# Two layers of a streaming encoder on one core: the adaLN sums, their buffers and the residual affine are placed anew

## The chip, the cores and the metric

The kernel runs on one core of one Trainium2 chip. The metric is the device time of one execution in microseconds. The engines are TensorE (PE in the profile; its weight loads are PEld), VectorE (DVE), ScalarE (ACT), GpSimd (POOL) and SyncE (SP), each with a queue of its own that it works through in order. DMAs are issued from such a queue too: a DMA whose buffer isn't free yet holds everything behind it on that queue.

## The reference

Two layers over 512 tokens of width 1024, all in float32. In each layer three sublayers follow one another, and each is modulated by a vector `c`:

```python
mod = (c_act @ ada_w[l] + ada_b[l]).reshape(b, N_SUB, 3, 1, D_MODEL)
h = modulate(x, mod[:, 0, 0], mod[:, 0, 1])              # x * (1 + scale) + shift
y = swiglu_ffn(h, ffn1_w_in[l], ffn1_w_out[l])
x = layer_norm(ALPHA * x + 0.5 * mod[:, 0, 2] * y, ln_g[l, 0], ln_b[l, 0])
...
x = layer_norm(ALPHA * x + mod[:, 1, 2] * y, ln_g[l, 1], ln_b[l, 1])
...
x = layer_norm(ALPHA * x + 0.5 * mod[:, 2, 2] * y, ln_g[l, 2], ln_b[l, 2])
```

The first and the third sublayer are SwiGLU networks with an inner width of 2816, the "half-steps". The second is a mixer of three head groups: a Mamba-2 scan, an attention with forgetting, and a gated short convolution. What `mod` gives each sublayer, shift, scale and gate, comes from a product of `silu(c)` with `ada_w`, 1024 by 9216 in each layer.

## The kernel before

**Sections.** The six sublayers are the sections 0 to 5; 0, 2, 3 and 5 are FFNs (`ffn`), 1 and 4 mixers (`mixer`). The residual stream `xt` stays in SBUF as four tiles of 128 tokens; its modulated and transposed form `hT` is the operand of the projections.

**Products in three passes.** Every float32 product is made of three float32r matmuls (`mm3`): each operand is split into a high part (ACT copies it: `hi`, `hh`, `ah`, `gh`) and a low part (VectorE subtracts: `li`, `hl`, `al`, `gl`). Weights are loaded as raw tiles (`ri`, `ro`, SyncE's queue, two buffers) and split into six high and six low tiles.

**An FFN** runs over 11 pairs of 256 inner columns, in a group of six and one of five. In a pair `cols_unit` loads and splits the weights of gate and of up, then four banks of 24 matmuls each follow (`order`), then `sg` (SiLU, ACT), `af` (product, VectorE), and `ah`, `al`, which stay in the pool `lp` (28 slots, tag "s") until the output projection. After each group `out_proj` multiplies them with the output weights in two halves `h`, and `fold` adds the gated result to `xt`. In the last group the layer norm follows tile by tile, and the next section's `hT` is made by transposes.

**The residual affine.** The norm leaves `xt` without its gain and bias, which the modulation has folded into `modA` and `modB`. For the residual, `x_affine` (line 632) multiplies all four tiles by `lng` and adds `lnb`, 16 instructions of 128x512 on POOL. It runs after pair 1 of an FFN, and in the mixer after `feat(C_C)`. `ln_vectors` (line 364) loads the four vectors, spread over the partitions, from ACT's queue. In section 0 the small parameter rows (`rows_v`, `rows_ln`) follow on the same queue; `columns` transposes them after pair 3 into `vT` and `lnT`.

**adaLN beside the FFN.** The product with `ada_w` is not done on TensorE but on VectorE, beside the FFN. `ada_acc` (line 228) loads eight blocks of 128x1024 (`ra`, pool `adap`, two buffers) and accumulates them in `acc`, weighted by `cT`. `acc_split` (line 246) splits the sum; the high halves `gh` lie in the temporaries `tp` (nine), the low ones `gl` in an `ra` buffer. `acc_sum` (line 257) then sums over the partitions by two matmuls with a matrix of ones, into a bank of the pool `psb` (four banks): `pm` for shift and scale, `pg` for the gate. `ada_ss(s)` makes the scale of section `s` (called `ss<s>.1` below) and its shift (`ss<s>.0`), `ada_gate(s)` its gate (`g<s>`).

These are generators. `begin` puts them in a list: in sections 0 and 3 the gate of the section, then `ss` and gate of the next one, then `ss` of the one after; in sections 2 and 5 the gate and, in 2, `ss` of section 3. `tick` is called twice in each pair, once after the weights of gate and once after those of up, both before the pair's matmuls, and once for each weight unit in `out_proj`. Each tick adds 2.7 credits (sections 0 and 3) or 1.3, and each block takes one. A generator that yields `TICK` ends the tick at once; so split and sum come at different ticks. `drain` runs what is left at a section's end.

**What sets the order.** The program only gives priorities: the framework's scheduler puts the instructions of each engine in an order by its own estimate of when they are ready. `issue_after` (used by `after`) adds a rule of order between two instructions of one engine. `mm_last` is the last instruction of the newest `mm3`.

**The mixer** uses the temporaries for its short-lived tiles: `am` (made on POOL, line 948), `cbm`, `m`, `xw`, `yo`, `prob`, `qa`, the high and low halves `pth` and `ptl`. Its projections (`feat`, 48 matmuls) are put between the steps of the scan and of the attention. It also takes two `ra` buffers for `xdt`.

Of the kernel before, what the change touches and what calls it, by code (L numbers as in the profile page):

```python
# [9 lines left out]
F32R = mybir.dt.float32r  # L10
# [5 lines left out]
P = 128  # L16
# [9 lines left out]
RMS_EPS = 1e-5  # L26
NEG = -1.0e30
NLONG = 28
NTMP = 9
NW = 6  # L30
PAD_W = 16
POS = 1
BPOS = 2
TICK = object()
CR = (2.7, 1.3)
WSZ = 1024

# [32 lines left out]
def trunk(ctx, tc, x, c, ln_in_g, ln_in_b, ada_w, ada_b, ffn1_w_in, ffn1_w_out,  # L70
# [11 lines left out]

    shift("pad0", PAD_W)
    rawp = ctx.enter_context(tc.tile_pool(name="rawp", bufs=2))
    adap = ctx.enter_context(tc.tile_pool(name="adap", bufs=2))
    whp = ctx.enter_context(tc.tile_pool(name="whp", bufs=NW))
    wlp = ctx.enter_context(tc.tile_pool(name="wlp", bufs=NW))
    lp = ctx.enter_context(tc.tile_pool(name="lp", bufs=NLONG))
# [15 lines left out]
    def tmp(shape, name, dt=F32):  # L104
        return tp.tile(shape, dt, tag="t", name=name)
# [30 lines left out]

    def rows_v(l):
        rows = slot([NROW, P], F32, f"rows{l}")
        act.dma_start(rows[0:72, :], ada_b[l].rearrange("(r p) -> r p", p=P))
        act.dma_start(rows[R_CW:R_CB, :], ssd_conv_w[l].rearrange("k (c p) -> (k c) p", p=P))  # L140
        act.dma_start(rows[R_CB:R_SW, :], ssd_conv_b[l].rearrange("(c p) -> c p", p=P))
        act.dma_start(rows[R_SW:R_NG, :], sconv_w[l].rearrange("k (c p) -> (k c) p", p=P))
        act.dma_start(rows[R_NG:NROW, :], ssd_norm_g[l].rearrange("(c p) -> c p", p=P))
        return rows

    def rows_ln():
        rows = slot([96, P], F32, "rowsl")
        act.dma_start(rows[0:48, :], ln_g.rearrange("l j (r p) -> (l j r) p", p=P))
        act.dma_start(rows[48:96, :], ln_b.rearrange("l j (r p) -> (l j r) p", p=P))
        return rows  # L150

    def rows_first():
# [93 lines left out]
    def acc_split(acc):  # L246

        parts = []
        los = adap.tile([P, 2, 512], F32R, tag="ra", name="gl")
        for h in range(2):  # L250
            hi, lo = tmp([P, 512], "gh", F32R), los[:, h]
            act.activation(hi, acc[h], AF.Copy)
            dve.tensor_tensor(lo, acc[h], hi.bitcast(F32), ALU.subtract)
            parts.append((hi, lo))
        return parts

    def acc_sum(ps, hi, lo):

        pe.matmul(ps, onesr, hi, start=True, stop=False)
        pe.matmul(ps, onesr, lo, start=False, stop=True)  # L260

    def new_mod(s):
# [21 lines left out]
    def ada_ss(s):  # L284
        l, j = divmod(s, 3)
        new_mod(s)
        pres = []
        for which in (1, 0):
            acc = None
            for a in ada_acc(l, (j * 3 + which) * D):  # L290
                acc = acc if a is TICK else a
                yield a
            sums = sm.tile([P, KD], F32, tag=f"sums{which}", name=f"sums{which}", bufs=1)
            parts = acc_split(acc)
            yield TICK
            for h in range(2):
                ps = pb([P, 4, P], f"pm{s}_{which}_{h}")
                acc_sum(ps, *parts[h])
                dg = tmp([P, 4, P], "dg")
                dve.tensor_tensor(dg, ps, ident[:, None, :].to_broadcast([P, 4, P]), ALU.mult)  # L300
                dve.tensor_reduce(sums[:, h * 4:h * 4 + 4], dg, axis=AX.X, op=ALU.add)
            pres.append(sums)
        mod_finish(s, 0, KD, *pres)

    FIRST = ((0, 4), (4, 3), (7, 1))
# [40 lines left out]
    def ada_gate(s):  # L346
        l, j = divmod(s, 3)
        col = (j * 3 + 2) * D
        gate = [slot([P, 512], F32, f"gate{s}_{h}") for h in range(2)]
        for h in range(2):  # L350
            sp.dma_start(gate[h], ada_b[l, col + h * 512:col + h * 512 + 512].partition_broadcast(P))
        acc = None
        for a in ada_acc(l, col):
            acc = acc if a is TICK else a
            yield a
        parts = acc_split(acc)
        yield TICK
        for h in range(2):
            ps = pb([P, 512], f"pg{s}_{h}")
            acc_sum(ps, *parts[h])  # L360
            dve.tensor_tensor(gate[h], ps, gate[h], ALU.add)
        gates[s] = gate

    def ln_vectors(s):
        g, b = (ln_in_g, ln_in_b) if s == 0 else (ln_g[(s - 1) // 3, (s - 1) % 3], ln_b[(s - 1) // 3, (s - 1) % 3])
        for n, v in (("g", g), ("b", b)):
            for h in range(2):
                a = slot([P, 512], F32, f"ln{n}{s}_{h}")
                act.dma_start(a, v[h * 512:(h + 1) * 512].partition_broadcast(P))
                aff[s, n, h] = a  # L370

    pending = []
# [3 lines left out]
    def begin(*gens):  # L376
# [2 lines left out]
        credit[0] = 0.0  # L379
        credit[1] = len(pending) and CR[0] if len(gens) > 2 else CR[1]  # L380

    def tick():
        credit[0] += credit[1]
        while pending and credit[0] >= 1:
            try:
                if next(pending[0]) is TICK:
                    break
                credit[0] -= 1
            except StopIteration:
                pending.pop(0)  # L390

# [237 lines left out]
        last[0] = act_last[0]  # L629
        return banks, units[2]  # L630

    def x_affine(s, eng):

        ln_vectors(s)
        for t in range(NT):
            for h in range(2):
                xh = xt[t][:, h * 512:(h + 1) * 512]
                eng.tensor_tensor(xh, xh, aff[s, "g", h], ALU.mult)  # L638
                eng.tensor_tensor(xh, xh, aff[s, "b", h], ALU.add)
# [17 lines left out]
    def by_token(ah, al):  # L657
        return lambda t: (ah[:, t * P:(t + 1) * P], al[:, t * P:(t + 1) * P])

    def ffn(s, w_in, w_out):  # L660
        for gi, grp in enumerate((range(0, 6), range(6, NPAIR))):
            acts = []
            for jp in grp:
                units, banks = [], []
                for which in range(2):
                    if s > 0 or jp > 0:
                        units.append(next_unit if (s, jp, which) == (0, 1, 0) else cols_unit(w_in, which * DFF + jp * 256, f"i{s}_{jp}_{which}", ln_done[0] if s > 0 and jp == 1 else None))
                        banks.append([pa([P, T], f"pf{s}_{jp}_{which}_{j}") for j in range(2)])
                    tick()
                if s == 0 and jp == 0:  # L670
                    banks, order = first_banks, []
                elif jp == 0:
                    order = [(0, KD, a, a + 256, j, which) for a in (0, 256) for which in range(2) for j in range(2)]
                else:
                    order = [(0, KD, 0, T, j, which) for j in range(2) for which in range(2)]
                for i, (ka, kb, a, b, j, which) in enumerate(order):
                    wh, wl = units[which][j]
                    for k in range(ka, kb):
                        mm3(banks[which][j][:, a:b], wh[:, k, :], wl[:, k, :],
                            hT[0][:, k, a:b], hT[1][:, k, a:b], k == 0, k == KD - 1)  # L680
                    if jp == 0 and i == POS:
                        last_tile[0](mm_last[0])
                for j in range(2):
                    sg = tmp([P, T], "sg")
                    act.activation(sg, banks[0][j], AF.Silu)
                    af = tmp([P, T], "af")
                    dve.tensor_tensor(af, sg, banks[1][j], ALU.mult)
                    ah = slot([P, T], F32R, f"ah{s}_{jp}_{j}")
                    al = slot([P, T], F32R, f"al{s}_{jp}_{j}")
                    act_last[0] = act.activation(ah, af, AF.Copy)  # L690
                    dve.tensor_tensor(al, af, ah.bitcast(F32), ALU.subtract)
                    acts.append(by_token(ah, al))
                if jp == 1:
                    x_affine(s, pool)
                    if s == 0:
                        masks()
                        rows = [(vT[0], rows_v(0)), (vT[1], rows_v(1)), (lnT, rows_ln())]
                        small_loads(0)
                        small_loads(1)
                if s == 0 and jp == 3:  # L700
                    for r in rows:
                        columns(*r)
                    neg_a()
            last = gi == 1
            if last:
                if s == 5:
                    ln_vectors(6)
            out_proj(s, w_out, grp[0] * 256, acts, True, not last, last)

    def out_proj(s, w_out, r0, acts, half, first, last):  # L710
# [6 lines left out]
        for h in range(2):  # L717
# [11 lines left out]
            for k in range(nhead):  # L729
                for t in range(NT):  # L730
                    go((k,), banks[t], t)
            for t in range(NT):
                if h == 1 and end == (s, t):
                    for piece in range(2):
# [465 lines left out]
```

## Time and profile before

| what | value |
|---|---|
| median of 3 runs | 2000.05 us (1996.82 to 2003.78) |
| the profiled execution | 2000.76 us, span 1999.0 us |
| granted TensorE clock, mean | 0.995 |
| bytes read from HBM | 260.37 MB |

The span runs from the first to the last instruction of the profiled execution. TensorE's share of busy time is high in every slice, so the views to read are those that show where it stands still: the list of its waits, the timeline at each of them, and windows of a few microseconds, which also give the clock that the throttle granted. One tick of work lasts long enough for a place to be named: in sections 0 and 3 a pair of undisturbed matmuls takes about 22 us. Section 0 reaches to about 418 us, mixer 1 to about 650, section 2 to about 1016, section 3 to about 1397, mixer 4 to about 1628; section 5 is the rest.

### The profile page before, as it was taken

To read this page: it belongs to the slowest core of one execution; us is meant where nothing else is said; L and a number is where in the kernel's file an instruction comes from. 1 tells how busy PE (TensorE), PEld (TensorE's weight loads), DVE (VectorE), ACT (ScalarE), POOL (GpSimd) and SP (SyncE) were. 2 spreads that over 40 slices of the span, in tenths; PEclk is the share of its full clock that TensorE was granted. 3 is DMA by queue.
4 is the path that set the end of the run, shared out by engine and by line. 5 is a ranking of instruction groups with operands and counts; after the bars stand their busy time and mean duration, and the time that the engine had idled before them with its cause. 6 is when DMAs were issued, how large, how long until landed. Compare 5 with 4: busy or idle time off the path is not lost.

```text
span 1999.0 us, 23434 instructions
## 1 busy us (share of the span) xinstructions
PE 1947.5 (97%) x9422; PEld 1627.3 (81%) x9422; DVE 1208.1 (60%) x1770; ACT 690.9 (35%) x1094; POOL 220.6 (11%) x182
## 2 busy tenths in 40 slices
PE   5999999999999999999999999999999999999998
PEld 4777878898878988888898788788978798888887
DVE  8886663477677655543477857435766785433336
ACT  3433223164365432123152322223544553222320
POOL 0230000007100040000005000000260004000000
PEclk9999999999999999999999999999999999999999
DMA  9766542234211544432345746232422144323331
GB/s 327 235 196 225 173 166 82 75 106 127 84 65 53 184 153 163 155 107 93 106 151 188 248 163 229 86 103 57 135 87 83 53 133 142 105 85 106 104 107 43
DMA packets 178605, 263.99 MB, mean 132 GB/s; under 512 B 9676, under 2 KB 124736, under 8 KB 178496
## 3 DMA queue, kind: packets, MB, share of 16 engines
q1 hardware_dynamic: 174000, 254.98, 38.8%
q10 hardware_dynamic: 4496, 7.52, 1.3%
q8 instruction: 74, 1.21, 0.2%
q14 instruction: 35, 0.29, 0.0%
HBM read 260.37 MB, written 2.10 MB: 131 GB/s over the span
## 4 chain that ended last, share of the span: by engine, by line
PE 77%; DVE 11%; DMA 7%; ACT 3%; issue 2%; POOL 0%; POOLq 0%; ACTq 0%; SPq 0%; DVEq 0%
PE pf L53 37%; PE po L53 23%; DMA ra<-in_ada_w_dram 6%; DVE acc L53 4%; PE pz L53 2%; DVE li L53 2%; DVE af L53 1%; PE pjm4x L53 1%; PE pjm1x L53 1%; PE ptr L53 1%; PE pS L53 1%; DMA ri<-in_ffn_w_in_dram 1%; PE py L53 1%; DVE x L53 1%; DVE gy L53 1%
## 5 line engine op out<-in xcount | busy, mean ns | idle before, releaser
L53 PE MATMUL pf<-hh,li 128*128 128x512 f32 (+1 forms) x1504 | 567.8, 378 | 1.4 <-DVE li L53 1.0
L53 PE MATMUL pf<-hl,hi 128*128 128x512 f32 (+1 forms) x1504 | 566.9, 377 | 0.2 <-DVE hl L53 0.2
L53 PE MATMUL pf<-hh,hi 128*128 128x512 f32 (+1 forms) x1504 | 566.9, 377 | 0.0
L53 DVE TENSOR_TENSOR li<-ri,hi 128x1024 fp32r<-128x1024 f32 x176 | 224.7, 1282 | 184.0 <-ACT hi L53 183.8
L53 PEld LDWEIGHTS pf<-hh,li 128*128 128x128 f32 x1504 | 284.4, 189 | 53.4 <-DVE li L53 1.7
L53 PEld LDWEIGHTS pf<-hl,hi 128*128 128x128 f32 x1504 | 284.2, 189 | 52.2 <-DVE hl L53 0.9
L53 PEld LDWEIGHTS pf<-hh,hi 128*128 128x128 f32 x1504 | 284.5, 189 | 51.3
L53 ACT ACTIVATE hi<-ri 128x1024 fp32r<-128x1024 f32 x176 | 185.5, 1060 | 311.1 <-PE pf L53 200.7
L53 PE MATMUL po<-ho,al 128*128 128x512 f32 (+1 forms) x704 | 273.5, 389 | 0.5 <-DVE af L53 0.4
L53 PE MATMUL po<-lo,ah 128*128 128x512 f32 (+1 forms) x704 | 272.9, 388 | 0.0
L53 PE MATMUL po<-ho,ah 128*128 128x512 f32 (+1 forms) x704 | 272.6, 388 | 0.0
L53 DVE TENSOR_TENSOR lo<-ro,ho 128x1024 fp32r<-128x1024 f32 x104 | 127.2, 1223 | 204.5 <-ACT ho L53 204.4
L53 DVE SCALAR_TENSOR_TENSOR acc<-ra,cT,acc 128x512 f32<-128x512 f32 x224 | 172.9, 815 | 67.1 <-DMA ra<-in_ada_w_dram 66.7
L53 ACT ACTIVATE ho<-ro 128x1024 fp32r<-128x1024 f32 x104 | 110.1, 1059 | 286.7 <-PE po L53 160.1
L451 POOL TENSOR_TENSOR rs<-ve,mhalf 128x1 f32<-128x1 f32 x28 | 17.3, 620 | 1277.5 <-DVE ve L53 1276.2
L53 PEld LDWEIGHTS po<-ho,al 128*128 128x128 f32 x704 | 132.2, 188 | 28.2 <-DVE af L53 0.8
L53 PEld LDWEIGHTS po<-ho,ah 128*128 128x128 f32 x704 | 132.2, 188 | 27.0
L53 PEld LDWEIGHTS po<-lo,ah 128*128 128x128 f32 x704 | 132.2, 188 | 26.9
L53 ACT ACTIVATE sg<-pf 128x512 f32<-128x512 f32 x88 | 52.4, 596 | 287.9 <-PE pf L53 270.7
L53 DVE TENSOR_TENSOR af<-sg,pf 128x512 f32<-128x512 f32 x88 | 60.1, 684 | 143.6 <-PE pf L53 141.0
L53 ACT ACTIVATE hf<-ptr,modB,modA 128x128 f32<-128x128 f32 (+1 forms) x168 | 67.0, 491 | 97.6 <-PE ptr L53 84.1
L638 POOL TENSOR_TENSOR x<-x,lng 128x512 f32<-128x512 f32 x48 | 75.5, 1598 | 218.7 <-DMA lng<-in_ln_g_dram 214.7
(397 smaller groups left out, 2488.3 us busy)
## 6 DMA issues: line engine op xcount, KB each, us to landing
ri<-in_ffn_w_in_dram SPq DMA_DIRECT2D x88, 1024.0 KB, 5.1
ra<-in_ada_w_dram SPq DMA_DIRECT2D x128, 512.0 KB, 3.9
ro<-in_ffn_w_out_dram SPq DMA_DIRECT2D x40, 1024.0 KB, 4.9
ro<-in_mix_w_out_dram SPq DMA_DIRECT2D x8, 1024.0 KB, 4.9
rf<-in_ada_w_dram SPq DMA_DIRECT2D x8, 512.0 KB, 8.4
ro<-in_ffn_w_out_dram SPq DMA_DIRECT2D x8, 512.0 KB
rf<-in_ada_w_dram SPq DMA_DIRECT2D x16, 192.0 KB, 6.5
gate<-in_ada_b_dram SPq DMA_DIRECT2D x12, 256.0 KB, 5.5
```

Of the source, the lines that this page charges most:

```text
L53: ins = f(*a, **k)
L451: pool.tensor_tensor(rs, ve, mhalf[:, 0:1], ALU.pow)
L638: eng.tensor_tensor(xh, xh, aff[s, "g", h], ALU.mult)
```

## The change

It does five things. The pool of `ra` gets a third buffer, and the low halves of a split go to the temporaries, which become seven instead of nine. A generator can yield `LATE` where it is ready to sum: the tick ends, and `resume` takes it on in the middle of the next pair's matmuls, or after the first step of an output projection's half 0; a further tick does the same if it comes first. A sum's first matmul is put after `mm_last`. The DMAs of the parameter rows and of the affine's vectors are issued from POOL's queue. And in the FFNs the affine runs on VectorE, one tile after each of the pairs 1 to 4; in the mixers it stays on POOL.

```diff
-NTMP = 9
+NTMP = 7
...
+LATE = object()
...
-    adap = ctx.enter_context(tc.tile_pool(name="adap", bufs=2))
+    adap = ctx.enter_context(tc.tile_pool(name="adap", bufs=3))
...
     def rows_v(l):
         rows = slot([NROW, P], F32, f"rows{l}")
-        act.dma_start(rows[0:72, :], ada_b[l].rearrange("(r p) -> r p", p=P))
...
+        pool.dma_start(rows[0:72, :], ada_b[l].rearrange("(r p) -> r p", p=P))
...
     def acc_split(acc):
 
         parts = []
-        los = adap.tile([P, 2, 512], F32R, tag="ra", name="gl")
         for h in range(2):
-            hi, lo = tmp([P, 512], "gh", F32R), los[:, h]
+            hi, lo = tmp([P, 512], "gh", F32R), tmp([P, 512], "gl", F32R)
...
     def acc_sum(ps, hi, lo):
 
-        pe.matmul(ps, onesr, hi, start=True, stop=False)
+        after(pe.matmul(ps, onesr, hi, start=True, stop=False), mm_last[0])
         pe.matmul(ps, onesr, lo, start=False, stop=True)
...
(ada_ss)
             parts = acc_split(acc)
-            yield TICK
+            yield LATE
             for h in range(2):
...
             pres.append(sums)
+            if which:
+                yield TICK
...
(ada_gate)
         parts = acc_split(acc)
         yield TICK
+        yield LATE
         for h in range(2):
...
(ln_vectors)
-                act.dma_start(a, v[h * 512:(h + 1) * 512].partition_broadcast(P))
+                pool.dma_start(a, v[h * 512:(h + 1) * 512].partition_broadcast(P))
...
+    late = [False]
+
     def tick():
         credit[0] += credit[1]
+        late[0] = False
         while pending and credit[0] >= 1:
             try:
-                if next(pending[0]) is TICK:
+                got = next(pending[0])
+                late[0] = got is LATE
+                if got is TICK or got is LATE:
                     break
                 credit[0] -= 1
+            except StopIteration:
+                pending.pop(0)
+
+    def resume():
+
+        if late[0]:
+            late[0] = False
+            try:
+                next(pending[0])
             except StopIteration:
                 pending.pop(0)
...
-    def x_affine(s, eng):
-
-        ln_vectors(s)
-        for t in range(NT):
+    def x_affine(s, eng, tiles=range(NT)):
+
+        if tiles[0] == 0:
+            ln_vectors(s)
+        for t in tiles:
...
(ffn, in the loop over the banks of a pair)
+                    if i == len(order) // 2 - 1:
+                        resume()
...
(ffn, after the pair)
+                if 0 < jp <= NT:
+                    x_affine(s, dve, (jp - 1,))
                 if jp == 1:
-                    x_affine(s, pool)
                     if s == 0:
                         masks()
...
(out_proj, after step k of half h)
+                if k == 0 and h == 0:
+                    resume()
```

More of the change, by code (lines that the diff above doesn't have):

```diff
@@ L138, in rows_v @@
         rows = slot([NROW, P], F32, f"rows{l}")
-        act.dma_start(rows[0:72, :], ada_b[l].rearrange("(r p) -> r p", p=P))
[L140 to L143, printed above, removed]
+        pool.dma_start(rows[0:72, :], ada_b[l].rearrange("(r p) -> r p", p=P))
+        pool.dma_start(rows[R_CW:R_CB, :], ssd_conv_w[l].rearrange("k (c p) -> (k c) p", p=P))
+        pool.dma_start(rows[R_CB:R_SW, :], ssd_conv_b[l].rearrange("(c p) -> c p", p=P))
+        pool.dma_start(rows[R_SW:R_NG, :], sconv_w[l].rearrange("k (c p) -> (k c) p", p=P))
+        pool.dma_start(rows[R_NG:NROW, :], ssd_norm_g[l].rearrange("(c p) -> c p", p=P))
         return rows
@@ L147, in rows_ln @@
         rows = slot([96, P], F32, "rowsl")
-        act.dma_start(rows[0:48, :], ln_g.rearrange("l j (r p) -> (l j r) p", p=P))
-        act.dma_start(rows[48:96, :], ln_b.rearrange("l j (r p) -> (l j r) p", p=P))
+        pool.dma_start(rows[0:48, :], ln_g.rearrange("l j (r p) -> (l j r) p", p=P))
+        pool.dma_start(rows[48:96, :], ln_b.rearrange("l j (r p) -> (l j r) p", p=P))
         return rows
```

## The prediction

> **What bounds the kernel now.** I read the page's first block first, then the list of waits of the matmul engine, then its timeline at each long wait, then five-microsecond windows around them.
>
> ```profile
> span 1999.0 us, 23434 instructions
> PE 1947.5 (97%) x9422; PEld 1627.3 (81%) x9422; DVE 1208.1 (60%) x1770; ACT 690.9 (35%) x1094; POOL 220.6 (11%) x182
> PE pm L53 <- ACT gh L53: 8.0, 4, 2.5
> PE pss L53 <- DVE xw L53: 4.2, 4, 1.4
> PE pm L53 <- DVE vT L53: 3.2, 1, 3.2
> PE pf L53 <- DVE li L53: 1.0, 1, 1.0
> PE pg L53 <- DVE gl L53: 0.5, 1, 0.5
> PE pg L53 <- ACT gh L53: 0.2, 1, 0.2
> PE pm L53 <- DVE gy L53: 0.3, 1, 0.3
> ```
>
> TensorE is busy 97% of the span: only time in which it stands still, or runs below its clock, can be won without removing matmuls, and the change removes none. Of its idle 51 us the rows on `pm` and `pg`, the adaLN sums over partitions, hold 8.0 + 3.2 + 0.5 + 0.2 + 0.3 = 12.2 us. The weights hardly ever keep it waiting (`pf <- li`, 1.0 us). The sums' larger waits one by one, where the bracket is TensorE's idle time before the instruction:
>
> ```profile
> 130.75 0.79 PE L53 MATMUL pm<-gh,onesr 128*128 128x512 f32 x1 [3.24 <-DVE vT L53]
> 159.34 0.50 PE L53 MATMUL pm<-gh,onesr 128*128 128x512 f32 x1 [1.53 <-ACT gh L53]
> 274.62 0.50 PE L53 MATMUL pm<-gh,onesr 128*128 128x512 f32 x1 [1.82 <-ACT gh L53]
> 1133.30 0.78 PE L53 MATMUL pm<-gh,onesr 128*128 128x512 f32 x1 [2.12 <-ACT gh L53]
> 1252.18 0.51 PE L53 MATMUL pm<-gh,onesr 128*128 128x512 f32 x1 [2.50 <-ACT gh L53]
> ```
>
> After three of them the clock falls too. The windows (busy time of each engine, then granted clock, DMA share, GB/s):
>
> ```profile
> 125.00:130.00 5.00, 2.50 (x13) 1.72 (x11) 4.61 (x7) 3.78 (x5) 0.00 (x0) 0.98 0.53 180
> 130.00:135.00 5.00, 4.25 (x10) 3.38 (x11) 4.96 (x13) 2.22 (x4) 0.00 (x0) 0.50 0.80 253
> 135.00:140.00 5.00, 5.00 (x20) 4.01 (x20) 4.23 (x8) 0.69 (x1) 0.00 (x0) 0.83 0.72 199
> 1130.00:1135.00 5.00, 2.88 (x10) 1.93 (x9) 4.49 (x8) 2.33 (x4) 0.00 (x0) 0.83 0.19 34
> 1135.00:1140.00 5.00, 5.00 (x19) 4.01 (x19) 4.57 (x11) 0.25 (x1) 0.00 (x0) 0.82 0.84 294
> 1250.00:1255.00 5.00, 2.81 (x8) 2.28 (x9) 4.24 (x8) 1.86 (x3) 0.00 (x0) 0.78 0.00 0
> 1255.00:1260.00 5.00, 5.00 (x21) 4.08 (x20) 4.41 (x7) 1.55 (x2) 0.00 (x0) 0.88 0.01 3
> 100.00:150.00 50.00, 46.76 (x196) 38.10 (x195) 44.59 (x55) 16.06 (x22) 15.32 (x9) 0.93 0.63 196
> 350.00:400.00 50.00, 50.00 (x222) 41.40 (x222) 21.78 (x29) 8.54 (x10) 0.55 (x1) 1.00 0.27 75
> ```
>
> Lost clock, as 5 us times what is missing to 1: 5 x (0.02 + 0.50 + 0.17) = 3.45; 5 x (0.17 + 0.18) = 1.75; 5 x (0.22 + 0.12) = 1.7: together 6.9 us. A check by counts: 222 matmuls fill an undisturbed 50 us (0.225 us each) and 196 ran from 100 to 150, so 26 x 0.225 = 5.9 us went there, against 3.24 + 3.45 = 6.7. **What the adaLN sums cost is 12.2 + 6.9 = 19.1 us.** This is the ceiling of the first three parts of the change.
>
> The Trainium skill, TensorE: Matmul & The Clock Gate, section "Why this matters for your kernels", says that the clock drops only after idle gaps above about 3 us. The trace disagrees: gaps of 2.12 and 2.50 us are followed by clocks of 0.83 and 0.78. By the page the sum would be 12.2 + 3.45 = 15.7; by the rows it is 19.1.
>
> **Third `ra` buffer, low halves in `tp`.** The two `ra` buffers are what the column blocks of `ada_w` stream through, and `acc_split` takes one of them from the split until the sum has run on TensorE:
>
> ```profile
> SPq L234 <- PE pg L53: 32.7, 5, 9.0
> SPq L234 <- PE pm L53: 31.9, 8, 9.0
> DVE acc L53 <- DMA ra<-in_ada_w_dram: 68.1, 45, 3.8
> ```
>
> The first two rows (SyncE's queue held at an `ra` load until a sum releases the buffer) go entirely, since no low half sits there any more: 64.6 us less holding, while loads have three buffers instead of one or two. VectorE's 68.1 us of waiting for `ra` in 45 pieces shrinks. So each accumulator ends earlier, by more than the 1.5 to 2.5 us by which the four `pm <- gh` sums were late. Bounds for those four: nothing won, or all 8.0 us plus their clock of 1.75 + 1.7. I take all, as 9.0 us of holding before a load is far more than 2.5 us of lateness.
>
> **Where the sums are issued.** I followed the credits (2.7 a tick in sections 0 and 3) through the generators. Splits come at the same ticks as before, in section 0: pair 2 first tick, pair 3 second, pair 5 first, first output projection unit 2 of both halves, pair 7 first. A tick clears the flag, so only a split at a pair's second tick lives to reach `resume`, or a gate's at the first, which takes one tick more. So `g0` moves from the second tick of pair 2 to its middle, `ss1.1` from the first tick of pair 4 to the middle of pair 3, section 3 likewise; `ss1.0` and `ss2.0`, which with section 3's are the four late ones, keep the second tick of their pair and get only the new order after the last matmul of the pair before. They therefore rest on the third buffer alone. The 3.24 us wait had another cause: three transposes `pv` and two sums ask for five of four `psb` banks at one place, and VectorE frees the bank only with `vT`. Half a pair now separates them: 3.24 + 3.45 us go.
>
> A sum in the middle of pair 3 can be early instead. Everything behind it on TensorE's queue waits:
>
> ```profile
> 122.98 1.35 ACT L53 ACTIVATE gh<-acc 128x512 fp32r<-128x512 f32 x2 [4.90 <-DVE acc L53]
> 126.08 0.37 PE L53 MATMUL pv_vT<-ident,rows 122*128 122x122 f32 x2
> ```
>
> Pair 3 ended at 126.08, so its middle, 48 matmuls earlier, was at about 115.3, and `gh` came at 122.98: it has to come 8 us earlier. Freeing the buffer (9.0) and VectorE (next part) does that, with little to spare. Bounds: 0 to two repeats of 3.24 + 3.45, 13.4 us. I charge 2 us, nearer to nothing.
>
> **Residual affine on VectorE.** 96 instructions on POOL (two rows of 48) belong to six sections; four FFN sections move, 64 instructions.
>
> ```profile
> L639 POOL TENSOR_TENSOR x<-x,lnb 128x512 f32<-128x512 f32 x48 | 81.4, 1721 | 0.2
> L53 DVE TENSOR_TENSOR x<-x,gy 128x512 f32<-128x512 f32 (+1 forms) x33 | 21.5, 671 | 0.5
> 91.25 3.44 DVE L53 SCALAR_TENSOR_TENSOR acc<-ra,cT,acc 128x512 f32<-128x512 f32 x2
> 116.39 1.40 DVE L53 SCALAR_TENSOR_TENSOR acc<-ra,cT,acc 128x512 f32<-128x512 f32 x2
> ```
>
> At the 671 ns of the like addition, VectorE gets 4 x 0.67 = 2.7 us after each of pairs 1 to 4, 10.7 us a section. Against that, two `acc` steps take 3.44 us while POOL runs its affine and 1.40 us just after: about 1 us for each instruction under POOL's stretch of 16 x 1.7 = 27 us. That is at least ten instructions, so VectorE comes out even; behind the affine stand the next `li`, which TensorE needs only a pair later (wait 1.0 us in all today). On the end: 0. Uncovered it would be at most 2.7 us a pair.
>
> **DMAs to Pool's queue.** ACT loses the issues:
>
> ```profile
> 96.63 0.60 ACT L53 ACTIVATE sg<-pf 128x512 f32<-128x512 f32 x1 [13.11 <-DMA ra<-in_ada_w_dram]
> L53 ACTq DMA_DIRECT2D lng<-in_ln_g_dram x12: 334/344/450, 454.9 to 1937.1; - x12
> lng<-in_ln_g_dram ACTq DMA_DIRECT2D x12, 256.0 KB, 3.6
> ```
>
> The 13.11 us in which ACT stood behind the row loads cost TensorE nothing (no wait there), so nothing is won on the end. VectorE now waits for `lng` if it reaches the affine too early: 3.6 us of landing plus four issues, at 0.34 us each on ACT; what POOL takes no row shows. From 0 to about 8 us a section, hidden by the weights split a pair ahead: 0.
>
> **Seven temporaries instead of nine.** In the FFN a split holds four until its sum, leaving three for `sg`, `af`, `gy`: enough. In the mixer:
>
> ```profile
> 483.23 1.03 POOL L948 TENSOR_TENSOR am<-a12h,upper 128x512 fp32r<-128x512 f32 x1
> 492.08 1.04 POOL L948 TENSOR_TENSOR am<-a12l,upper 128x512 fp32r<-128x512 f32 x1 [2.83 <-PE pd L53]
> 491.61 0.39 PE L53 MATMUL pd<-am,slowr 128*128 128x512 f32 x1
> ```
>
> POOL builds five `am` before the first `pd` at 491.61, then waits for a release. With seven, the first `ssd_decay` (cbm, four `am`, two `m`) fills them all, and the second starts only after that `pd`: some 2 to 4 us later. Projections (48 matmuls, 10.8 us each) lie around it as filler. Bounds 0 to 12 us a mixer; I charge 1 us each, 2 us.
>
> **The sum.** -19.1 + 2 + 2 = -15.1. The profiled execution took 2000.76 us (span 1999.0 and 1.76 around it), so 1985.7 by it; the median of the runs is 0.7 lower: **1985.0**.
>
> **Rivals.** *The sums stay late* (the change doesn't do what it says): the four `.0` sums keep their tick, so if VectorE, not the buffer, sets when the accumulator ends, 8.0 + 3.45 us stay; only 7.7 us of the 19.1 go: 2000 - 7.7 = 1992.4. For it: VectorE is busy 44.59 of 50 us from 100 to 150. Against it: the 64.6 us of held loads. *The mixers pay* (slower): with seven temporaries each mixer's decay and its four attention blocks, which want `qa`, four `prob` and two pairs of `pt`, lose 2 to 4 us at some four places, 12 us a mixer, when the filler projections are used up. It decides the sign above (19.1 - 2) / 2 = 8.6 us a mixer; at 12: 2000 - 17.1 + 24 = 2007. For it: `pss <- xw` already waits 4.2 us, so there the filler is thin. *They cancel*: both by half, within 0.3%: about 1997.
>
> The Trainium skill, SBUF — State Buffer, section "Who interferes with whom", has a DMA from POOL's queue starved of descriptors while VectorE holds the shared port. No DMA of before is on that queue. In the mixer it would delay POOL's affine and the `am` behind it; that is the slower rival's place, and its price is kept there.
>
> **Chances.** Forecast (1979 to 1990) 0.55; sums stay late 0.2; cancel 0.13; mixers pay 0.12. Range 1979 to 1998: the forecast with all 19.1 and a little noise at the low end, the late sums and most of the cancelling. A measurement tells 0.3%, 6 us, from no change: faster 0.73, same 0.15, slower 0.12.
>
> **What would show it.** Right: no `pm` or `pg` wait above 0.5 us, granted clock 1.00 after 100, no `ra` load held for a `pm`, `acc` steps of 0.7 us throughout pair 2. Wrong: `pm <- gh` waits at the middle of pair 3 or at the start of pairs 5 and 7; more than 2 us of new TensorE waits between 430 and 640; VectorE waiting for `lng` and `li` late behind it.

## The result, and the profile after

The changed kernel takes **2033.39 us** (median of 4 runs, 2031.63 to 2034.54), against 1999.34 us of the kernel before on the same chip (4 runs, 1996.82 to 2003.78). The ratio is **1.0167, 95% interval [1.0147, 1.0187]**: slower by some 33 us, where 15 us faster was forecast, and outside the range. The profiled execution took 2032.67 us, its span 2030.9 us.

The list of TensorE's waits in the profile after (total us, times, longest):

```profile
PE pcs L54 <- DVE a L54: 20.8, 2, 10.5
...
PE pf L54 <- DVE hl L54: 7.7, 4, 3.0
...
PE pm L54 <- ACT gh L54: 4.0, 2, 3.4
PE pv L54 <- DVE hl L54: 3.1, 2, 1.6
...
PE pm L54 <- DVE gy L54: 2.6, 2, 1.9
...
PE pd L54 <- POOL am L971: 2.4, 4, 0.7
```

Some of these rows are new. `pcs <- a` is the first product of the mixers' decay chain and stood in no list before; `pf <- hl` is the start of an FFN section and had 0.2 us; `pd <- am`, the small wait of the mixers that seven temporaries were to bring, is new as well. The `pm` rows, which the change was to clear, fell from 8.0 + 3.2 + 0.3 to 4.0 + 2.6 us.

Where in the span the time went is seen from the section ends (the end of a section is taken as the last of the four `rs <- ve` on POOL, a step of the layer norm):

| section | before, us | after, us | difference |
|---|---|---|---|
| 0 (to its end) | 418.5 | 413.6 | -4.9 |
| 1, mixer | 234.2 | 250.3 | +16.1 |
| 2 | 366.6 | 368.5 | +2.0 |
| 3 | 378.3 | 377.3 | -1.1 |
| 4, mixer | 234.2 | 250.9 | +16.7 |
| 5 (to the same place) | 360.9 | 363.9 | +2.9 |

Half of the loss lies in each mixer, in which the change touches only the queue of four loads, the number of temporaries and, by `xdt`, the `ra` buffers. POOL's timeline in mixer 1, after:

```profile
413.55 0.55 POOL L468 TENSOR_TENSOR rs<-ve,mhalf 128x1 f32<-128x1 f32 x1 [7.21 <-DVE ve L54]
...
414.52 1.26 POOL L372 DMA_DIRECT2D lng<-in_ln_g_dram  x2
415.77 1.07 POOL L372 DMA_DIRECT2D lnb<-in_ln_b_dram  x2
418.72 5.41 POOL L656 TENSOR_TENSOR x<-x,lng 128x512 f32<-128x512 f32 x3 [1.89 <-DMA lng<-in_ln_g_dram]
...
442.54 1.26 POOL L657 TENSOR_TENSOR x<-x,lnb 128x512 f32<-128x512 f32 x1
```

and the same work before, first the issue in ACT's timeline, then POOL's:

```profile
454.93 0.78 ACT L53 ACTIVATE cv<-pjm1c,vT 128x512 f32<-128x512 f32 x1 [1.16 <-PE pjm1c L53]
454.94 0.35 ACTq L53 DMA_DIRECT2D lng<-in_ln_g_dram  x1
```

```profile
458.19 8.32 POOL L638 TENSOR_TENSOR x<-x,lng 128x512 f32<-128x512 f32 x5 [38.69 <-DMA lng<-in_ln_g_dram]
...
481.10 2.16 POOL L639 TENSOR_TENSOR x<-x,lnb 128x512 f32<-128x512 f32 x1
```

The code place is the same, but ACT reached the loads only after all the copies ahead of them in its queue. POOL has nothing to do there and issues them at once, **40.4 us earlier** (414.52 against 454.94), which is 35.5 us earlier counted from the start of the section. So the affine, which waits for nothing but them, moves from 458 to 483 us forward to 419 to 444 us. What VectorE does in that stretch is the chain of small steps that leads to `a`. Four of its groups from 434 to 446 us, before and then after (count, busy us and mean ns of one, idle us):

```profile
L53 DVE SCALAR_TENSOR_TENSOR ppl<-ppl,z 128x48 f32<-128x48 f32 x7 | 1.5, 208 | 0.2
L53 DVE RECIPROCAL av<-av 128x48 f32<-128x48 f32 x1 | 0.5, 453 | 0.0
L53 DVE TENSOR_TENSOR z<-zz 128x48 f32<-128x48 f32 x1 | 0.2, 209 | 0.0
L53 DVE TENSOR_SCALAR ppl<-z 128x48 f32<-128x48 f32 x1 | 0.2, 187 | 0.0
```

```profile
L54 DVE SCALAR_TENSOR_TENSOR ppl<-ppl,z 128x48 f32<-128x48 f32 x7 | 5.5, 786 | 0.2
L54 DVE TENSOR_TENSOR z<-zz 128x48 f32<-128x48 f32 x1 | 1.2, 1185 | 0.0
L54 DVE TENSOR_SCALAR ppl<-z 128x48 f32<-128x48 f32 x1 | 1.2, 1166 | 0.0
L54 DVE RECIPROCAL av<-av 128x48 f32<-128x48 f32 x1 | 0.5, 453 | 0.0
```

Steps of 0.2 us take up to 1.2 us, about as long as one of POOL's instructions (1.26 us, the row at 442.54). The Trainium skill, SBUF — State Buffer, section "Who interferes with whom", states that a VectorE instruction with two SBUF inputs contends with a GpSimd instruction that reads SBUF, and that the one that comes second is blocked for the whole of the other. The rows of the two-input steps (`ppl<-ppl,z`, and `z<-zz`, which reads `zz` twice) agree; the one-input `ppl<-z` was slowed as well, which that sentence doesn't cover. The prediction took the starving of POOL's DMAs from that section, and it was this other sentence of it that decided.

TensorE's timeline at the end of the chain, and windows around it (busy us of PE, PEld, DVE, ACT, POOL, then granted clock, DMA share, GB/s):

```profile
445.47 0.60 PE L54 MATMUL pcs<-a,upper 128*128 128x32 f32 x2 [10.48 <-DVE a L54]
```

```profile
440.00:445.00 5.00, 0.00 (x0) 0.00 (x0) 4.72 (x9) 0.00 (x0) 3.73 (x4) 0.51 0.00 0
445.00:450.00 5.00, 4.53 (x21) 4.56 (x22) 1.99 (x9) 0.92 (x2) 4.06 (x4) 0.50 0.00 0
450.00:455.00 5.00, 5.00 (x30) 5.00 (x29) 3.58 (x5) 0.61 (x1) 0.00 (x0) 0.63 0.01 3
```

TensorE waits 10.48 us, and the clock is 0.50 and 0.63 in the ten microseconds behind the wait: 5 x (0.50 + 0.37) = 4.4 us more. With 1.6 us of `pv <- hl` shortly before, that makes about 16.5 us, against the 16.1 us that this mixer lost.

### The profile page after: what moved, and what is told of

The parts are those of the page before. It is cut to its first block, busy times and chain, and to the rows that moved or that the text cites. A ratio compares the mean times of both kernels' runs of the same rounds, so it can differ in the third digit from the quotient of the medians.

```text
span 2030.9 us, 23452 instructions
## 1 busy us (share of the span) xinstructions
PE 1954.2 (96%) x9422; PEld 1633.6 (80%) x9422; DVE 1228.6 (60%) x1834; ACT 691.8 (34%) x1094; POOL 135.9 (7%) x158
## 4 chain that ended last, share of the span: by engine, by line
PE 80%; DVE 10%; DMA 5%; ACT 2%; issue 1%; POOL 1%; POOLq 0%; DVEq 0%; SPq 0%; ACTq 0%
PE pf L54 41%; PE po L54 24%; DMA ra<-in_ada_w_dram 4%; PE pz L54 2%; DVE acc L54 1%; DVE li L54 1%; PE pjm1x L54 1%; PE pjm4x L54 1%; DMA ri<-in_ffn_w_in_dram 1%; DVE x L54 1%; DVE af L54 1%; DVE hl L54 1%; PE pS L54 1%; DVE ppl L54 1%; PE py L54 1%
## 5 line engine op out<-in xcount | busy, mean ns | idle before, releaser
L54 DVE TENSOR_TENSOR li<-ri,hi 128x1024 fp32r<-128x1024 f32 x176 | 214.2, 1222 | 189.0 <-ACT hi L54 188.8
L54 DVE SCALAR_TENSOR_TENSOR acc<-ra,cT,acc 128x512 f32<-128x512 f32 x224 | 155.8, 745 | 48.7 <-DMA ra<-in_ada_w_dram 48.5
L54 ACT ACTIVATE ah<-af 128x512 fp32r<-128x512 f32 x88 | 54.3, 619 | 36.2 <-DVE af L54 34.4
```

The costliest lines, as they stand in the source:

```text
L54: ins = f(*a, **k)
```

## The experiments

The theory on the **mixers** (number 1 where an expectation counts): the loads' new queue lets the affine start too early. The theory on the **FFN sections** (number 2) was first that the third buffer's loads make the `hl` waits; it fell, and in its place came the theory that the FFN's vector loads, too, start too early on POOL's idle queue. Each ratio is to the kernel before on the same chip.

| run | us | ratio, 95% interval |
|---|---|---|
| the changed kernel | 2033.39 | 1.0167 [1.0147, 1.0187] |
| e1: mixers' loads on ACT | 2001.38 | 1.0006 [0.9989, 1.0024] |
| e2: before, mixers' loads on POOL | 2031.9 | 1.015 [1.0124, 1.0177] |
| e3: before, seven temporaries | 2000.49 | 0.9997 [0.9983, 1.0011] |
| e4: no affine in the mixers | 2005.95 | one run |
| e5: e1, two `ra` buffers | 2017.03 | 1.0085 [1.0069, 1.01] |
| e6: e1, first ticks after the last tile | 1989.65 | 0.9951 [0.9936, 0.9966] |
| e7: e6, sums by `resume` only | 1990.21 | 0.9958 [0.9943, 0.9972] |
| e8: e7, one tick more before a sum | 1981.74 | 0.9911 [0.9897, 0.9926] |
| e9: all vector loads on ACT | 1987.77 | 0.9946 [0.9929, 0.9962] |
| e10: e8, all vector loads on ACT | 1980.65 | 0.9908 [0.989, 0.9925] |
| e11: e8, FFN affine on POOL | 2022.03 | 1.0116 [1.0098, 1.0134] |
| e12: before, FFN loads on POOL | 2017.72 | 1.0092 [1.0076, 1.0109] |
| e13: e10, FFN affine on POOL | 1985.62 | 0.9929 [0.9915, 0.9944] |
| e14: e9, FFN affine on POOL | 1995.32 | 0.9987 [0.9975, 0.9998] |
| e15: e9, two `ra` buffers | 2005.79 | 1.0039 [1.0022, 1.0056] |

### The mixers

**e1**, the changed kernel with the mixers' loads back on ACT's queue:

```diff
-                pool.dma_start(a, v[h * 512:(h + 1) * 512].partition_broadcast(P))
+                (act if s % 3 == 1 else pool).dma_start(a, v[h * 512:(h + 1) * 512].partition_broadcast(P))
```

> The changed kernel, but in the two mixers the affine's four vectors are loaded from ACT's queue again. Theory 1 (POOL's queue lets the mixer's affine start some 40 us earlier, and it then takes VectorE's time from the decay chain for which TensorE waits at pcs): the two pcs waits of 10.5 us go, each mixer falls from 250 to about 235 us, the whole to about 2003 us (1999 to 2007). Rival (seven temporaries lengthen the mixers, as the prediction's slower rival had it): the mixers stay at 250, the whole at 2030 to 2035.

**e2**, the kernel before with this part alone, `(pool if s % 3 == 1 else act)` in the same line:

> The kernel before, with one edit alone: in the two mixers the affine's four vectors are loaded from POOL's queue. Theory 1: each mixer goes from 234 to about 250 us with a pcs wait of some 10 us, the whole to 2025 to 2033 us. Rival (temporaries): as before, 1996 to 2003 us.

**e3**, the kernel before with `NTMP = 7`:

> The kernel before with seven temporaries instead of nine, nothing else. Theory 1: the mixers stay at 234 us, or gain at most 2 each, the whole 1996 to 2004 us. Rival (temporaries): each mixer some 8 to 16 us longer, the whole 2015 to 2031 us.

**e4**, the changed kernel without the mixers' affine:

```diff
-        x_affine(s, pool)
+        ln_vectors(s)
```

> The changed kernel without the 16 affine instructions of each mixer: there the residual keeps no gain and bias; the four loads stay on POOL's queue. Theory 1 (it is the affine's instructions that slow VectorE): no pcs wait, VectorE's small steps of the decay chain at 0.2 us again, mixers at 232 to 236 us, the whole about 2000 us. Rival (POOL writing the descriptors of its own DMAs slows VectorE): the pcs waits stay, the whole at about 2030 us.

In e1 the `pcs` waits are gone and the mixers take 234.4 and 235.7 us. In e2, which has nothing else of the change, they are back:

```profile
452.42 0.60 PE L53 MATMUL pcs<-a,upper 128*128 128x32 f32 x2 [10.48 <-DVE a L53]
```

with mixers of 249.6 and 249.8 us. One line of one kind of load is thus worth +0.015 x 2000 = 30 us by itself, and (1.0167 - 1.0006) x 2000 = 32 us within the change. e4 has the loads at their early place on POOL, but no affine behind them: no `pcs` wait, mixers of 234.4 and 235.9 us. So it is POOL's arithmetic and not its DMAs that VectorE pays for. e3 clears the temporaries: mixers of 234.4 and 235.5 us, no difference that can be measured. The wait `pd <- am` is there in e3 too, 2.4 us in 4, but `pss <- xw` falls from 4.2 to 1.0 us.

### The FFN sections

e1 should have kept the forecast gain and only reached the time of before; its FFN sections have `pf <- hl` waits of 7.1 us in 4. **e5** is e1 with `bufs=2` for `adap`; **e6** is e1 with the first pair's ticks behind the last tile of `hT`, so that the `acc` steps stand behind the last `hl` in VectorE's order:

```diff
-                    tick()
+                    if s == 0 or jp > 0:
+                        tick()
...
                         last_tile[0](mm_last[0])
+                        tick()
+                        tick()
```

> Run e1 with two ra buffers again (the low halves stay in the temporaries). Theory 2 (with the third buffer the scheduler puts a fourth block's accumulation ahead of the last tile's hl on VectorE's queue, where it waits for its DMA, and TensorE waits at hl): the hl waits of about 2 us at the start of sections 2, 3 and 5 fall below 1 us, sections 2 and 5 return from 370.7 and 365.2 to 366 to 368 and 361 to 362 us; some of the sums' waits in sections 0 and 3 return; the whole 1992 to 2002 us. Rival (the affine on VectorE makes hl late): the hl waits stay at 2 us, sections 2 and 5 at 370 and 365.

> Run e1 with three buffers, and the two ticks of pair 0 in sections 2, 3 and 5 taken after the last tile's modulation is issued, so that the accumulations of the first blocks get a lower priority than its hl. Theory 2: the three hl waits go with their clock, sections 2 and 5 at 366 and 361 us, section 3 about 3 us shorter; the whole 1988 to 1993 us. Rival: no change against e1, 2001 us.

e5 keeps the `hl` waits (2.4 us the longest) with two buffers: the theory that the third buffer makes them fell. It also shows what the buffer is for, since `pm <- gh` is back at 11.6 us in 7. e6 has no `pf <- hl` wait above 0.2 us and is 0.0055 x 2000 = 11 us below e1. That showed where the wait arises, not why it hadn't been there before the change, when the same order cost 0.2 us. VectorE's timeline at the start of section 3, after:

```profile
1038.09 0.68 DVE L54 TENSOR_TENSOR hl<-hf,hh 128x512 fp32r<-128x512 f32 x1
1044.25 1.42 DVE L54 SCALAR_TENSOR_TENSOR acc<-ra,cT,acc 128x512 f32<-128x512 f32 x2 [5.48 <-DMA ra<-in_ada_w_dram]
1045.58 0.68 DVE L54 TENSOR_TENSOR hl<-hf,hh 128x512 fp32r<-128x512 f32 x1
```

The last `hl` stands behind an `acc` step that waits 5.48 us for its block, and TensorE waits 3.03 us for the `hl` (the longest in the list of waits). Here, too, the affine's loads had moved: they issue at 1033.20 us, 0.8 us behind the section's start. **e9** puts all of `ln_vectors` back on ACT, the parameter rows stay on POOL:

```diff
-                pool.dma_start(a, v[h * 512:(h + 1) * 512].partition_broadcast(P))
+                act.dma_start(a, v[h * 512:(h + 1) * 512].partition_broadcast(P))
```

> The changed kernel with all six sections' affine vectors loaded from ACT's queue again (the row loads stay on POOL's). Theory (POOL's idle queue starts these loads too early, in the mixers and in the FFN sections): the mixers' waits on pcs (10.4 us each) go as with the mixers' loads alone, and the waits pf <- hl at the start of sections 2, 3 and 5 (1.81, 3.03, 2.67 us after) fall to 1 us or less, since the FFN's loads issue some 30 us later: sections 2 and 5 near 366.5 and 361 us instead of 368.5 and 363.9; total 1986 to 1994. Rival (in the FFN sections the queue does not matter, VectorE's order does): hl waits stay at 1.5 to 3 us, total as with the mixers' loads alone, 1998 to 2004.

**e12** is the kernel before with the FFN sections' loads alone on POOL, `(act if s % 3 == 1 else pool)`:

> The kernel before with one part of the change alone: the FFN sections' vector loads (four a section, 1 MB) from POOL's queue, the mixers' on ACT's as before. Theory (queue of the loads): they issue at the sections' start, compete with ra and ri there, and pf <- hl waits of 1.5 to 3 us appear in sections 2, 3 and 5 (0.7 us before); POOL's affine at pair 1 stays where it is: 2004 to 2012. Rival (order on VectorE makes those waits, not the queue): no hl wait above 1 us, 1996 to 2003.

e9 came out as the theory had it, 1987.77 us. Its VectorE at the same place:

```profile
1017.33 0.69 DVE L54 TENSOR_TENSOR hl<-hf,hh 128x512 fp32r<-128x512 f32 x1
1018.27 1.41 DVE L54 SCALAR_TENSOR_TENSOR acc<-ra,cT,acc 128x512 f32<-128x512 f32 x2 [0.25 <-DMA ra<-in_ada_w_dram]
1019.60 0.69 DVE L54 TENSOR_TENSOR hl<-hf,hh 128x512 fp32r<-128x512 f32 x1
```

The wait of 5.48 us is 0.25 us. The DMAs of the 20 us in which that happens, after (1030 to 1050) and then e9 (1008 to 1028): KB each, and the median time from issue to landing.

```profile
ra<-in_ada_w_dram SPq DMA_DIRECT2D x5, 512.0 KB, 8.4
ri<-in_ffn_w_in_dram SPq DMA_DIRECT2D x2, 1024.0 KB, 7.1
lng<-in_ln_g_dram POOLq DMA_DIRECT2D x2, 256.0 KB, 4.0
lnb<-in_ln_b_dram POOLq DMA_DIRECT2D x2, 256.0 KB, 6.7
```

```profile
ra<-in_ada_w_dram SPq DMA_DIRECT2D x7, 512.0 KB, 4.7
ri<-in_ffn_w_in_dram SPq DMA_DIRECT2D x2, 1024.0 KB, 5.5
```

A block of `ada_w` takes 8.4 us beside the four loads and 4.7 us without them. The Trainium skill, DMA: Bandwidth & Descriptors, section "Issuing engines are not separate DMA queues", states that DMAs started from any engine's queue run on the same 16 DMA engines and interleave; the two rows of `ra` agree. In the changed kernel this costs (1.0006 - 0.9946) x 2000 = 12 us, by the two intervals uncertain by some 5 us; from e1 to e9 the sections 2, 3 and 5 get shorter by 4.2, 2.5 and 4.2 us.

e12 was off by more than its theory: 2017.72 us where 2004 to 2012 were expected. It adds what the changed kernel lacks, an affine on POOL that follows its loads to the section's start. POOL and then VectorE in section 2 of e12:

```profile
655.12 4.26 POOL L638 TENSOR_TENSOR x<-x,lng 128x512 f32<-128x512 f32 x3 [1.74 <-DMA lng<-in_ln_g_dram]
```

```profile
660.99 3.08 DVE L53 SCALAR_TENSOR_TENSOR acc<-ra,cT,acc 128x512 f32<-128x512 f32 x2 [4.03 <-DMA ra<-in_ada_w_dram]
663.99 1.74 DVE L53 TENSOR_TENSOR hl<-hf,hh 128x512 fp32r<-128x512 f32 x1
665.66 4.52 DVE L53 TENSOR_TENSOR li<-ri,hi 128x1024 fp32r<-128x1024 f32 x2
```

Both costs lie on one another there: `acc` waits 4.03 us for its block, then an `acc`, an `hl` and a `li` each take about double (two `li` 4.52 us, against 2.35 in the undisturbed order). I had kept the affine at pair 1, where the code has it; but the code place binds nothing on an engine that is otherwise idle.

### What is left of the change

**e14** is e9 with the FFN affine on POOL at pair 1, as before; of the change it keeps buffer, sums, temporaries and row loads. **e13** is the same edit on e10. **e15** is e9 with `bufs=2`.

```diff
-                if 0 < jp <= NT:
-                    x_affine(s, dve, (jp - 1,))
                 if jp == 1:
+                    x_affine(s, pool)
```

> The changed kernel with all vector loads on ACT's queue and the FFN affine on POOL at pair 1: of the change only the third buffer, the sums' places, the seven temporaries and the row loads are left. By the prediction's terms (buffer and sums -19.1 +2 +2, affine 0): as with the affine on VectorE, 1984 to 1992. If the affine's move is part of the gain: 1992 to 2002, sums late at pairs 3, 5 and 7.

> The changed kernel with all vector loads on ACT's queue (1987.8) and two ra buffers instead of three; the low halves stay in the temporaries. If the third buffer is what lets the accumulators end in time (the prediction's part one): pm <- gh waits of 1 to 4 us in sections 0 and 3, as in the run with two buffers and the FFN's loads on POOL's queue (11.6 us in all there), 1996 to 2006. If taking the low halves out of the two buffers was enough: 1986 to 1992.

> The version with all vector loads on ACT's queue and the sums' ticks moved (1980.65), with the FFN sections' affine on POOL at pair 1 as before. Unlike the run with loads on POOL's queue (2022.0), the loads now hold the affine back to about 43 us into the section, as in before. If the engine itself is worth nothing, as the prediction had it: 1976 to 1986. If POOL's stretch makes acc and li steps twice as long in pair 2 and the accumulators late: 1986 to 1998, with pm <- gh waits of 1 to 3 us in sections 0 and 3.

e14 fits the second of its two readings in time, 1995.32 us; of the sums that this reading named, only those of pair 3 are late. The affine's move is worth (0.9987 - 0.9946) x 2000 = 8 us, buffer and sums without it 0.0013 x 2000 = 3 us. By the section ends, e14 loses 6.0 us against e9 in section 0 and 2.1 us in section 3, where many accumulators run; sections 2 and 5 take the same time in both. The copy of the split that the sum in the middle of pair 3 waits for, in ACT's timeline of e14 and then of e9:

```profile
125.28 1.36 ACT L54 ACTIVATE gh<-acc 128x512 fp32r<-128x512 f32 x2 [4.73 <-DVE acc L54]
```

```profile
121.76 1.30 ACT L54 ACTIVATE gh<-acc 128x512 fp32r<-128x512 f32 x2 [1.13 <-DVE acc L54]
```

With POOL's 27 us of affine in pair 2 the accumulator ends 3.5 us later. TensorE's `pm` waits in e14 and in e9:

```profile
PE pm L54 <- ACT gh L54: 6.7, 2, 4.7
...
PE pm L54 <- DVE gy L54: 2.8, 2, 2.1
```

```profile
PE pm L54 <- DVE gy L54: 2.6, 2, 1.4
PE pm L54 <- ACT gh L54: 1.6, 2, 1.1
```

e13 is weaker evidence: 1985.62 us lies at the edge of its first reading ("worth nothing"), it has no `pm` wait, and its interval overlaps that of e10, 1980.65 us; (0.9929 - 0.9908) x 2000 = 4 us. By the section ends the difference is 5.1 us in section 0 and nothing elsewhere, and there TensorE waits at another place, `pf <- sg`, 3.1 us. e15 gives the third buffer (1.0039 - 0.9946) x 2000 = 19 us, as its first reading had it: with two, `pm <- gh` is 8.8 us in 6, and in all the kernel is slower than before. A likely reason, which no run separates, is that the sums come earlier than before and the accumulators don't.

**e11** made the move of e13 with the FFN loads still on POOL's queue:

> The best version so far (1981.7) with the FFN sections' residual affine on POOL in one stretch at pair 1, as before, instead of tile by tile on VectorE. If the move to VectorE is worth nothing, as the prediction had it: same within 0.3%, 1976 to 1988, VectorE's acc steps at twice their length during POOL's 27 us and short behind it. If POOL's stretch costs VectorE more than the 10.7 us a section it takes off: accumulators end later and pm <- gh waits of 1 to 3 us return in sections 0 and 3, with their clock: 1987 to 1996. If VectorE is relieved: 1974 to 1979.

None of its three readings held: 2022.03 us. The list of TensorE's waits:

```profile
PE pf L54 <- DVE af L54: 16.7, 2, 8.5
...
PE pf L54 <- DVE li L54: 13.3, 2, 12.2
```

As in e12 the affine starts with the section (648.88 us, 4.7 us behind its start), and now VectorE's steps for the first pair's products are late. The same edit costs some 4 us with the loads on ACT's queue (e13) and (1.0116 - 0.9911) x 2000 = 41 us with them on POOL's.

### Later sums

The rest of the `pm` waits is a matter of when a sum is issued. **e7** is e6 with `if late[0]: return` in place of `late[0] = False` in `tick`, so that only `resume` sums; **e8** adds a `yield TICK` ahead of `yield LATE` in `ada_ss`; **e10** is e8 with all vector loads on ACT.

> Run e6, and a tick doesn't take on a generator that is ready to sum: sums come from the middle of a pair (or from the output projection's first half) alone. Theory 3 (sums right at the start of pair 6 find no psb bank, since VectorE hasn't folded the output projection's banks yet): the two waits of about 1.5 us on gy go, 2 to 6 us less than e6; the whole 1983 to 1990 us. Rival (the sum is late wherever it stands, since VectorE is behind): the waits move to the middle of the pair, time as e6.

> Run e7, and between split and sum of shift and scale lies one tick more, as for the gate. Theory 4 (the sum of ss1.1 at the middle of pair 3 was too early by 1 to 3 us, which the prediction charged with 2): no pm wait over 0.5 us left, clock at 1.00 in sections 0 and 3, 1 to 4 us less than e7; the whole 1980 to 1988 us. Rival: half a pair between split and sum is enough, time as e7 within 2 us.

> The best version so far (mixers' loads on ACT, ticks after the last tile, one tick more before the sums; 1981.7) with the FFN sections' vector loads on ACT's queue too. Theory: the hl waits are gone there already, so at most the 0.5 to 1 us a section that VectorE waits less for ra at the section's start is left: 1979 to 1983. Rival: VectorE now reaches the affine before lng has landed (issue about 30 us later), holds the next li back, and pf <- li waits of over 1 us appear: 1984 to 1992.

e7 won nothing: it took the waits for `gy` away, but `pm <- gh` waits rose from 2.5 us in e6 to 4.4 us (2.08, 1.41 and 0.76 us the longest), as its rival had it. e8 has none above 0.5 us, and e10 none either; the two can't be told apart. From 100 to 150 us, where before had 196 matmuls, e10 has 224 at full clock:

```profile
100.00:150.00 50.00, 50.00 (x224) 41.37 (x223) 35.44 (x55) 18.70 (x24) 0.00 (x0) 1.00 0.52 182
```

e10, at **1980.65 us**, is the fastest kernel of this study: 0.9908 [0.989, 0.9925] of before.

## Why the prediction was wrong

**The ceiling of 19.1 us: right in size.** It added TensorE's waits on the sums and the clock lost behind them. e10, in which both are gone, is 0.0092 x 2000 = 18 us faster than before. The 15.7 us that the prediction worked out beside it lies within e10's interval too (15 to 22 us), so this total doesn't decide between the two; the rows of the clock in the last section do. For those 15.7 us the prediction took the 3 us of the Trainium skill, TensorE: Matmul & The Clock Gate, section "Why this matters for your kernels", as a bound below which the clock stays; that section advises against gaps above about 3 us. The rows in the last section show shorter gaps with a fallen clock.

**Third buffer: right.** No SyncE load is held for a sum any more, and the four `.0` sums wait nowhere after. It is worth 19 us in e15.

**Sum in the middle of pair 3: right in kind, too small.** The charge was 2 us within bounds of 0 to 13.4. In the changed kernel that sum waits 3.43 us and the clock falls to 0.66 in the next five, 3.43 + 1.7 = 5.1 us in section 0. With the affine on POOL the term is larger: e14's two `pm <- gh` waits are these sums, 6.7 us, and the clock is 0.58 and 0.66 in the five microseconds behind them, 5 x (0.42 + 0.34) = 3.8 us: 10.5 us. Its `pm <- gy` waits, 2.8 us, belong to the sum behind the output projection, a term that the prediction didn't have. I counted the freed buffer as 9 us of head start; the `gh` that had come at 122.98 came at 124.06 us, and at 121.76 us in e9.

That the wait stayed at 3.43 us was luck. The prediction put the sum at the pair's middle, 48 matmuls ahead of its end; TensorE's timeline after has it behind 368 of the first four pairs' 384 `pf` matmuls, only 16 ahead of the end. The order after `mm_last` lets the scheduler put it later, and it did. An estimate: 32 matmuls earlier, at the prediction's 0.225 us each, the sum would have waited 7.2 us more, some 10.6 us.

**Affine on VectorE "0 on the end": too small a gain.** The step set VectorE's own 10.7 us a section against what it is freed of, and called it even. Even in busy time isn't even in time of arrival: one accumulator at the place where a sum waits ends 3.5 us earlier, and the move is worth 8 us, all of it in sections 0 and 3 (some 4 us in the better kernel, where the intervals overlap).

**"DMAs to Pool's queue ... hidden: 0": this is the step that failed.** It counted what the issues cost (four at 0.34 us) and whether VectorE would come to the affine too soon. It did not ask when the loads would now *start*. On ACT they were held back by everything ahead of them in that queue, and that delay kept POOL's affine clear of the decay chain and the loads clear of the section's start. The rows for this were at hand in the profile before: the first `lng` issue of a mixer at 454.9 us, 36 us behind the section's start, and POOL standing idle for 38.69 us before its first affine instruction, released by `lng`. Measured: 32 us in the mixers and 12 us in the FFN sections.

**Seven temporaries, 2 us: nothing measurable** (e3). The forecast wait came, 2.4 us of `pd <- am`, and `pss <- xw` fell by 3.2 us. *The mixers pay* thus named the right place, at 2007 us, for a reason that was false. The starving of DMAs that stood beside it isn't what cost the time: `lng` lands 4.1 us after its issue on POOL (median of 12), against 3.6 us on ACT, and `lnb` 5.1 against 3.8 us; and e4, with these loads on POOL, has no `pcs` wait. Of the signs named in advance two came: "more than 2 us of new TensorE waits between 430 and 640", and a `pm <- gh` wait at pair 3.

**The terms as measured**, one after the other as ratios times 2000: buffer, sums, temporaries and rows -3 (e14), affine -8 (e9), FFN loads' queue +12 (e1), mixers' loads' queue +32: +33 us. With the affine's vectors left on ACT's queue (e9) the forecast of 1985 us would have met 1987.77 us, but in part by luck: buffer, sums and temporaries, forecast at -15.1 us, gave -3 us (e14), as 10.5 + 2.8 us of waits and clock stand at other sums there, and the affine, forecast at 0, gave the other -8 us.

## What to carry to other kernels

A DMA's place in a busy engine's queue is also a timer for all that waits on it; before it is moved to an idle queue, work out when it will start there, what its data releases, and what that will run beside. A statement on an engine with nothing else to do runs when its inputs land, not where it stands in the code, so work that contends is placed by a dependency. And a helper engine is priced by the arrival of the step that TensorE waits for next, not by a balance of busy time.

## What the runs showed of the hardware

The price of sharing falls on small VectorE steps most: 128x48 steps went from 208 to 786 ns in the mean, and `ppl<-z`, which has one input tile, from 187 to 1166 ns, while a RECIPROCAL of the same shape kept its 453 ns and the one-input `av<-ee` took 173 ns (both at 435 us, within POOL's stretch). The 128x1024 `li` only doubled (4.52 against 2.35 us for two).

The clock fell behind gaps shorter than 3 us here too, but the length of a gap alone doesn't decide. Two waits of e14, each with the five microseconds behind it:

```profile
247.14 0.47 PE L54 MATMUL pm<-gh,onesr 128*128 128x512 f32 x1 [2.07 <-DVE gy L54]
247.14:252.14 5.00, 5.00 (x22) 4.14 (x23) 5.00 (x9) 0.00 (x0) 0.00 (x0) 1.00 0.01 3
...
1102.80 0.67 PE L54 MATMUL pm<-gh,onesr 128*128 128x512 f32 x1 [1.97 <-ACT gh L54]
1102.80:1107.80 5.00, 5.00 (x15) 3.98 (x16) 4.02 (x6) 1.71 (x3) 0.00 (x0) 0.66 1.03 379
```

The longer gap left the clock at 1.00, the shorter brought it to 0.66. In the changed kernel gaps of 1.81 us (before 676.00) and 1.94 us (before 1240.40) left it at 1.00, and one of 3.03 us (before 1046.32) brought it down:

```profile
1045.00:1050.00 5.00, 3.68 (x22) 3.68 (x23) 5.00 (x7) 1.55 (x2) 0.00 (x0) 0.76 0.58 162
1050.00:1055.00 5.00, 5.00 (x40) 5.00 (x40) 5.00 (x8) 1.06 (x1) 0.00 (x0) 0.90 0.87 292
```

In the rows of before, 2.12 us brought it to 0.83. What decides besides the length isn't shown by these runs.

Issuing on POOL is dearer as well: 540 ns for a 256 KB load (median of 12), against 344 ns on ACT.
